# One attention loop over eight heads with a block of matmuls between any two steps, five PSUM banks for attention and three for the blocks

## The chip, the cores and the metric

The kernel runs on one core of one Trainium2 chip. The metric is the device time of the whole kernel in microseconds; three runs of the kernel before gave 1835.82 to 1836.56, median 1836.43.

## The reference, cut to the mixer

Two layers of an encoder run over 320 tokens: 256 of a prompt and 64 of a later step, side by side in one tile, in float32. A layer is SwiGLU, a mixer of three attentions, cross-attention to a memory, and a second SwiGLU, each with a layer norm behind it. The change touches the mixer:

```python
z = x @ w_in
(aq, ak, av, bq, bk, bv, iq, ik, iw, cq, ck, cv, gates) = split(z)
# A: chunk-band attention, 4 heads of 64, relative-position bias
ya = softmax(aq . ak / 8 + rel_bias) @ av
# B: top-k keys by the indexer's score, 4 heads of 64 on one shared K/V head
score = sum_h iw[h] * relu(iq[h] . ik);  sel = top_k(score)
yb = softmax(bq . bk[sel] / 8) @ bv[sel]
# C: differential attention, 4 heads of 2 x 64, headwise RMSNorm
a = softmax(cq[0] . ck[0] / 8) - lam * softmax(cq[1] . ck[1] / 8)
yc = rmsnorm(a @ cv) * subln_g * (1 - lam_init)
g_a, g_b, g_c = split(sigmoid(gates))
merged = g_a * (ya @ wb_a) + g_b * (yb @ wb_b) + g_c * (yc @ wb_c)
x = layer_norm(ALPHA * x + merged @ w_out)
```

## The kernel before, in words

A weight block is 128 x 1024 floats. `stream()` lists all blocks in the order of use. `nextw` hands out the next block and has `ahead(2)` prepare blocks until two more are ready: a DMA on SP's queue brings it into `raw`, ACT copies it to a rounded `hi` (L148), DVE subtracts to get `lo` (L151), both in two halves. `raw`, `hi` and `lo` have three buffers each. `block_mm` multiplies a block with the activations, which are split into high and low parts too: `mm3` (L183 to L185) issues three matmuls for each of eight pieces, so a block is 24 matmuls of 320 columns into one PSUM bank.

PSUM has eight banks. `psmm` takes from a group of four (`mm`, `PSM = 4`) for blocks, for the pairs of SwiGLU, for the memory's key and value projections that fill the norms (`fill_k`, `fill_v`), and for `proj_v`, which holds three at once. `psat` takes from the other four (`at`) for attention, for the norms' sums and for transposes. A bank is free again when ACT or DVE has read the tile.

The mixer (`attn_layer`) first projects values, indexer and the first keys and queries, computes the index scores, and then runs the loop. Eight steps of heads: two pairs of A heads, four C heads, two pairs of B heads. Each has scores (L633, two banks, then `softmax`: minima on DVE at L651 or L653, exp on ACT at L657, which for B and C heads reads the banks, a scaling on DVE at L665); a turn (L672, L674, L675: transposes into t0, t1 and `po`, three banks, read out at L681 to L683 or L818 and L819); values (L695 to L702 or L825 to L830, into `po`); for C heads a finish (L848, one bank, read at L851 and L852). Between the steps stand ten projections of queries and keys (`projs`, each with a rotation: L534 to L536 on DVE and POOL, L569 on POOL, and two steps of top-k, L777 and L778 on DVE) and six of the 24 gate blocks (`some_gates`, L787: tanh on ACT). Their order is written out by hand: some steps stand directly behind each other. The merge then goes over eight output blocks: three products of the branches with `wb` (A: 2 pieces, B: 2, C: 4), each scaled by its gate on DVE (L918), two adds on POOL (L919, L920), a split on ACT and DVE (L194, L195), and three more gate blocks behind each of the first six. Then comes the output projection (`wo`), whose results go into the residual (`Norm.resid`, L382 and L404), and with block 4 the norm starts its sums, between which `fill_k` or `fill_v` run; their results are read out late, at L298 or L328.

The program is laid out by a framework which fixes the order of each engine's instructions before the run, from the source's order and an estimate of when each can start, and places the semaphores. An engine then works its list strictly in order.

Of the kernel before, what the change touches and what calls it, by code (L numbers as in the profile page):

```python
# [10 lines left out]
F32 = mybir.dt.float32  # L11
# [42 lines left out]
QK1 = ([("aq", 0), ("ak", 0), ("aq", 1), ("ak", 1)]  # L54
       + [x for i in range(4) for x in (("cq", i), ("ck", i))] + [("bq", 0), ("bq", 1)])
QK = QK0 + QK1
EARLY = 2
TOPN = 2
NGATE = 10
NSLOT = 30  # L60
PSM = 4
FILL = ((8, 8, 4, 4), (4, 4, 0, 0))


def stream():
    for l in range(DEPTH):
        yield from ffn_stream(l, 0)
        for kc in range(4):
            yield ("wv0", l, kc), 656
        for q in QK0:  # L70
            yield ("wqk", l, QK.index(q)), D
        for h in range(4):
            yield ("wv1", l, h), D
        for q in QK1:
            yield ("wqk", l, QK.index(q)), D
        for g in range(EARLY * 3):
            yield ("wg", l, g), D
        for m in range(KB):
            yield ("wb", l, m), D
            for g in range((m + EARLY) * 3, min(m + EARLY + 1, KB) * 3):  # L80
                yield ("wg", l, g), D
        for n in ("wo", "wmq", "wmo"):
            for m in range(KB):
                yield (n, l, m), D
        yield from ffn_stream(l, 1)


def ffn_stream(l, which):
    for j in range(FB):
        for s in range(2):  # L90
            yield ("wgu", l, which, j, s), D
    for m in range(KB):
        for c0 in range(0, FB, 8):
            yield ("wd", l, which, m, c0), min(8, FB - c0) * 128
# [3 lines left out]
def encoder(ctx: ExitStack, tc: tile.TileContext, a):  # L98
# [29 lines left out]
    def psmm():  # L128
        return ps.tile([128, 512], F32, tag="mm", bufs=PSM, name="mm")

# [42 lines left out]
    def nextw(*key):  # L173
        ahead(1)
        k, w = ready.pop(0)
        assert k == key, (k, key)
        ahead(2)
        return w

    def mm3(out, w, x, k, kx, first, last):  # L180
# [124 lines left out]
    def fill_v(l, half):  # L305
        st = {}

        def mk(kc):
            def mm(w, ks):
                t = memT[0]  # L310
                if kc == 0 and 0 in ks:
                    st["p"] = [psmm() for _ in range(2)]
                for i in ks:
                    b, kk = i // 4, (i // 2) % 2
                    ts = slice(b * 128, (b + 1) * 128)
                    k = kc * 2 + kk
                    c = slice(kk * 512, (kk + 1) * 512)
                    p = st["p"][b]
                    if i % 2 == 0:
                        pe.matmul(p, t[:, 0, k, ts], w[0][:, c], start=(k == 0), stop=False)  # L320
                        pe.matmul(p, t[:, 1, k, ts], w[0][:, c], start=False, stop=False)
                    else:
                        pe.matmul(p, t[:, 0, k, ts], w[1][:, c], start=False, stop=(k == KB - 1))

                def out():
                    for b in range(2):
                        o = slot()[:, :512]
                        act.activation(o, st["p"][b], AF.Copy)  # L328
                        nc.sync.dma_start(a["omv"][l, :, b, half * 512:(half + 1) * 512], o)
                        c = half * D + b * 512  # L330
                        nc.sync.dma_start(mkv[l][:, 1, c:c + 512], o)
                if kc == 3 and 7 in ks:
                    late.append(out)
            return mm
        return [(a["wmv"][l, half * 4 + kc], mk(kc)) for kc in range(4)]
# [143 lines left out]
    def ffn(l, which, x, norm):  # L479
        h = []  # L480
        for j in range(FB):
            pg, pu = psmm()[:, :NT], psmm()[:, :NT]
            wg = nextw("wgu", l, which, j, 0)
            if j == 0 and not (l or which):
                for k in range(KB):
                    c = slice(k * 128, (k + 1) * 128)
                    pe.matmul(pg, wg[0][:, c], x[k][0], start=(k == 0), stop=False)
                    pe.matmul(pg, wg[0][:, c], x[k][1], start=False, stop=False)
                for k in range(KB):
                    c = slice(k * 128, (k + 1) * 128)  # L490
                    pe.matmul(pg, wg[1][:, c], x[k][0], start=False, stop=(k == KB - 1))
                wu = nextw("wgu", l, which, j, 1)
                for k in range(KB):
                    mm3(pu, wu, x, k, k, k == 0, k == KB - 1)
            elif j == 0:
                wu = nextw("wgu", l, which, j, 1)
                for k in range(KB):
                    mm3(pg, wg, x, k, k, k == 0, k == KB - 1)
                    mm3(pu, wu, x, k, k, k == 0, k == KB - 1)
            else:  # L500
                for k in range(KB):
                    mm3(pg, wg, x, k, k, k == 0, k == KB - 1)
                wu = nextw("wgu", l, which, j, 1)
                for k in range(KB):
                    mm3(pu, wu, x, k, k, k == 0, k == KB - 1)
            if l == 0 and which == 0 and j == 4:
                constants()
            if l == 0 and which == 0 and j == 6:
                load_mem()
            s = wtile()  # L510
            act.activation(s, pg, AF.Silu)
            dve.tensor_tensor(out=s, in0=s, in1=pu, op=OP.mult)  # L512
            h.append(pair())
            split(s, h[j])
        for m in range(KB):
            p = psmm()[:, :NT]
            for c0 in range(0, FB, 8):
                w = nextw("wd", l, which, m, c0)
                for k in range(min(8, FB - c0)):
                    mm3(p, w, h, k, c0 + k, c0 + k == 0, c0 + k == FB - 1)  # L520
            norm.resid(m, p)

    def attn_layer(l, x, norm):
# [255 lines left out]
                if not steps:  # L779
                    dve.tensor_scalar(hide, tk, MARK, None, op0=OP.is_gt)  # L780

        gates = []

        def gate(i):
            p = block_mm(nextw("wg", l, i), x)
            g = wk.tile([128, NT], F32, tag="gate", bufs=NGATE, name="gate")
            act.activation(g, p, AF.Tanh, scale=0.5)  # L787
            gates.append(g)

        def a_scores(hp):  # L790
            s, _ = scores(qk["aq", hp], qk["ak", hp])
            return softmax(s, bias=toep[:, hp])
# [60 lines left out]

        rest = [q for q in QK1[4:]]

        def projs(n):
            for _ in range(n):
                proj(*rest.pop(0))
                topk(TOPN)

        ng = [0]

        def some_gates(n):
            for _ in range(n):
                gate(ng[0])
                ng[0] += 1

        e0, e1 = a_scores(0), a_scores(1)
        projs(2)
        p0 = turn2(e0)  # L870
        projs(1)
        a_values(0, *p0)
        p1 = turn2(e1)
        projs(1)
        a_values(1, *p1)
        e0 = c_scores(0)
        projs(2)
        e1 = c_scores(1)
        projs(1)
        p0 = c_turn(e0)  # L880
        projs(1)
        w0 = c_values(0, *p0)
        e2 = c_scores(2)
        projs(1)
        p1 = c_turn(e1)
        projs(1)
        w1 = c_values(1, *p1)
        c_finish(0, w0)
        e3 = c_scores(3)
        some_gates(1)  # L890
        p2 = c_turn(e2)
        some_gates(1)
        w2 = c_values(2, *p2)
        c_finish(1, w1)
        e0 = b_scores(0)
        p3 = c_turn(e3)
        some_gates(1)
        w3 = c_values(3, *p3)
        c_finish(2, w2)
        e1 = b_scores(1)  # L900
        some_gates(1)
        p0 = turn2(e0)
        some_gates(1)
        b_values(0, *p0)
        p1 = turn2(e1)
        c_finish(3, w3)
        some_gates(1)
        b_values(1, *p1)
        some_gates(EARLY * 3 - ng[0])
        mg = []  # L910
        for m in range(KB):
            w = nextw("wb", l, m)
            gm = gates[3 * m:3 * m + 3]
            for b, (k0, n) in enumerate(((0, 2), (2, 2), (4, 4))):
                p = psmm()[:, :NT]
                for k in range(k0, k0 + n):
                    mm3(p, w, o, k, k, k == k0, k == k0 + n - 1)
                dve.scalar_tensor_tensor(gm[b], gm[b], 1.0, p, op0=OP.add, op1=OP.mult)  # L918
            pool.tensor_tensor(out=gm[0], in0=gm[0], in1=gm[1], op=OP.add)  # L919
            pool.tensor_tensor(out=gm[0], in0=gm[0], in1=gm[2], op=OP.add)  # L920
            mg.append(pair())
            split(gm[0], mg[m])
            for i in range((m + EARLY) * 3, min(m + EARLY + 1, KB) * 3):
                gate(i)
        load_mem()
        for m in range(KB):
            norm.resid(m, block_mm(nextw("wo", l, m), mg))
# [306 lines left out]
```

## Time and profile before

| | |
|---|---|
| median of three runs | 1836.43 us |
| the profiled execution | 1840.81 us |
| its span, first to last instruction | 1839.0 us |
| PE busy | 1768.6 us, 96% |
| DVE busy | 1173.5 us, 64% |
| ACT busy | 866.6 us, 47% |
| POOL busy | 279.5 us, 15% |
| DMA | 277.60 MB, 151 GB/s |

PE is the engine of the matmuls, PEld its loading of weights, DVE the vector engine, ACT the scalar engine, POOL GpSimd; SP only issues DMAs. Busy time of PE is the union of its instructions, whose ends are modelled. PEclk is the granted clock of TensorE: 1.00 is 2.4 GHz and 0.50 is 1.2 GHz. In a timeline row the bracket says how long the engine had been idle and what ended that. Times are us from the first instruction.

Layer 0's attention loop lies at 336 to 438.6 us, its merge behind it to 530, its output projection from there to 579; layer 1's loop lies at 1253.8 to 1356.5.

### The profile page before, as it was taken

How to read it: one execution, taken by the hardware profiler on the slowest of the kernel's cores; microseconds unless marked ns; L12 is line 12 of the kernel's file. 1: busy time of each engine (PE TensorE's matmuls, PEld its weight loads, DVE VectorE, ACT ScalarE, POOL GpSimd, SP SyncE). 2: the span in 40 equal slices, each digit the busy share in tenths (PEclk: the TensorE clock that was granted, in tenths of full speed). 3: DMA queues.
4: the chain of work that ended last, by engine and by line, in shares of the span. 5: the costliest groups of instructions: out<-in, count | busy, mean ns of one | idle time of the engine just before them, and what ended most of it. 6: DMA issues, size and time to landing. Idle time of an engine off the chain costs nothing. (4 is left out here: it accounts for less than half of the span.)

```text
span 1839.0 us, 31561 instructions
## 1 busy us (share of the span) xinstructions
PE 1768.6 (96%) x12148; PEld 1714.2 (93%) x12148; DVE 1173.5 (64%) x2274; ACT 866.6 (47%) x1939; POOL 279.5 (15%) x311
## 2 busy tenths in 40 slices
PE   8999999989998989999999999999899999899997
PEld 8999999979997989999999999999799989799996
DVE  5544667976567786444674446679765786844455
ACT  5444445555444655443444444455554455544433
POOL 1000122231123030000210001222311230400012
PEclk9999999999999999999999999999999999899998
DMA  6545645433556544445544445554334563354443
GB/s 223 172 150 146 197 143 184 144 108 115 150 171 214 170 140 132 149 150 154 181 136 150 149 144 156 163 173 150 102 121 154 162 199 100 105 160 149 147 126 101
DMA packets 93015, 277.60 MB, mean 151 GB/s; under 512 B 12480, under 2 KB 26688, under 8 KB 92352
## 3 DMA queue, kind: packets, MB, share of 16 engines
q1 hardware_dynamic: 85376, 268.64, 47.0%
q10 hardware_dynamic: 7488, 6.95, 1.3%
q8 instruction: 95, 1.56, 0.4%
q14 instruction: 56, 0.46, 0.1%
HBM read 260.67 MB, written 14.55 MB: 150 GB/s over the span
## 5 line engine op out<-in xcount | busy, mean ns | idle before, releaser
L183 PE MATMUL mm<-slot,hi 128*128 128x320 f32 x3368 | 1051.2, 312 | 17.4 <-ACT slot L472 7.9
L185 PE MATMUL mm<-slot,hi 128*128 128x320 f32 x3368 | 1043.9, 311 | 3.0 <-DVE slot L474 3.0
L184 PE MATMUL mm<-slot,lo 128*128 128x320 f32 x3368 | 1045.5, 311 | 0.5 <-DVE lo L151 0.4
L151 DVE TENSOR_TENSOR lo<-raw,hi 128x512 fp32r<-128x512 f32 (+2 forms) x876 | 616.1, 742 | 349.5 <-ACT hi L148 346.7
L148 ACT ACTIVATE hi<-raw 128x512 fp32r<-128x512 f32 (+2 forms) x876 | 496.2, 613 | 569.5 <-issue 343.2
L183 PEld LDWEIGHTS mm<-slot,hi 128*128 128x128 f32 x3368 | 636.9, 189 | 26.6 <-ACT slot L472 9.9
L185 PEld LDWEIGHTS mm<-slot,hi 128*128 128x128 f32 x3368 | 635.3, 189 | 6.7 <-DVE slot L474 6.2
L184 PEld LDWEIGHTS mm<-slot,lo 128*128 128x128 f32 x3368 | 636.6, 189 | 1.9 <-DVE lo L151 1.4
L386 POOL TENSOR_TENSOR acc<-x 128x320 f32<-128x320 f32 x8 | 10.0, 1254 | 850.4 <-DVE x L382 850.4
L512 DVE TENSOR_TENSOR w<-w,mm 128x320 f32<-128x320 f32 x88 | 42.9, 488 | 132.1 <-PE mm L185 126.4
L787 ACT ACTIVATE gate<-mm 128x320 f32<-128x320 f32 x48 | 21.0, 438 | 75.2 <-PE mm L185 75.2
L444 POOL TENSOR_TENSOR x<-x,msb 128x320 f32<-128x320 f32 x47 | 46.1, 1012 | 53.6 <-ACT msb L430 53.6
L377 POOL TENSOR_TENSOR acc<-acc,w 128x320 f32<-128x320 f32 x40 | 45.9, 1148 | 45.4 <-ACT w L371 44.6
L535 POOL TENSOR_TENSOR w<-w,cst 128x320 f32<-128x320 f32 x30 | 27.0, 898 | 165.0 <-DVE w L534 110.9
L472 ACT ACTIVATE slot<-w,vec 128x320 fp32r<-128x320 f32 x56 | 34.4, 649 | 35.2 <-DVE w L461 35.2
L376 POOL TENSOR_TENSOR acc<-acc,x 128x320 f32<-128x320 f32 x32 | 34.7, 1085 | 80.9 <-DVE x L404 80.1
L371 ACT ACTIVATE w<-x 128x320 f32<-128x320 f32 x64 | 28.4, 465 | 35.9 <-DVE x L404 26.2
L918 DVE SCALAR_TENSOR_TENSOR gate<-gate,mm 128x320 f32<-128x320 f32 x48 | 22.7, 483 | 32.5 <-PE mm L185 32.5
L195 DVE TENSOR_TENSOR slot<-w,slot 128x320 fp32r<-128x320 f32 x88 | 42.7, 485 | 0.5 <-ACT slot L194 0.5
L919 POOL TENSOR_TENSOR gate<-gate 128x320 f32<-128x320 f32 x16 | 14.1, 879 | 190.8 <-DVE gate L918 190.8
L194 ACT ACTIVATE slot<-w 128x320 fp32r<-128x320 f32 x88 | 40.2, 457 | 3.3 <-DVE w L512 3.2
L657 ACT ACTIVATE e<-at,st 128x192 f32<-128x192 f32 (+4 forms) x60 | 24.3, 422 | 35.6 <-DVE st L651 28.7
(238 smaller groups left out, 1621.9 us busy)
## 6 DMA issues: line engine op xcount, KB each, us to landing
raw<-wgu SPq DMA_DIRECT2D x175, 512.0 KB, 3.5
raw<-wd SPq DMA_DIRECT2D x64, 512.0 KB, 3.6
raw<-wg SPq DMA_DIRECT2D x48, 512.0 KB, 3.5
raw<-wqk SPq DMA_DIRECT2D x38, 512.0 KB, 3.6
raw<-wd SPq DMA_DIRECT2D x32, 384.0 KB, 3.5
raw<-wmk SPq DMA_DIRECT2D x16, 512.0 KB, 3.9
raw<-wb SPq DMA_DIRECT2D x16, 512.0 KB, 3.5
raw<-wo SPq DMA_DIRECT2D x16, 512.0 KB, 3.6
```

The lines of the kernel that those rows point to most:

```text
L148: act.activation(hi[:, c], raw[:, c], AF.Copy)
L151: dve.tensor_tensor(out=lo[:, c], in0=raw[:, c], in1=f(hi)[:, c], op=OP.subtract)
L183: pe.matmul(out, hi[:, c], x[kx][0], start=first, stop=False)
L184: pe.matmul(out, lo[:, c], x[kx][0], start=False, stop=False)
L185: pe.matmul(out, hi[:, c], x[kx][1], start=False, stop=last)
L194: act.activation(dst[0], src, AF.Copy)
L195: (eng or dve).tensor_tensor(out=dst[1], in0=src, in1=f(dst[0]), op=OP.subtract)
L376: eng.tensor_tensor(out=self.acc1, in0=x32[0] if m == 1 else self.acc1, in1=x32[m], op=OP.add)
L377: pool.tensor_tensor(out=self.acc2, in0=self.sq0 if m == 1 else self.acc2, in1=sq, op=OP.add)
L444: eng.tensor_tensor(out=x32[m], in0=x32[m], in1=msb, op=OP.subtract)
L472: act.activation(x[m][0], u, AF.Identity, scale=g, bias=b)
L512: dve.tensor_tensor(out=s, in0=s, in1=pu, op=OP.mult)
```

## The change

The banks are divided three (`PSM = 3`) to five. `fill_v` and the second half of each SwiGLU pair take theirs from the attention's five; in the merge branch B's product does too. The loop over heads is a real loop now: for each head a block, the next head's scores, a block, this head's turn, a block, this head's values, and for a C head the finish one head later. The blocks come from one list, `MIX`: P is a projection with its two steps of top-k, G a gate; ten P and fourteen G, against ten and six before. The first six gates lie in pairs in the slots of the large pool, the others in ten buffers as before; `gates_by(m)` says how many gates stand behind each output block of the merge: one behind the first, three behind the third to fifth, none behind the others. The merge takes the branches in the order A, C, B. Where the block just handed out is of `wqk`, `wg` or `wb`, the next one is copied to `hi` and `lo` whole and not in halves.

```diff
-EARLY = 2
+SGATE = 6
+EARLY = 14
+MIX = "PPGPPGPGPPGPGPPG" + "G" * 8
-PSM = 4
+PSM = 3
+def gates_by(m):
+    return min(3 * KB, max(3 * (m + 1), SGATE) + NGATE - 1) if m >= 0 else EARLY
...
-        ahead(2)
+        ahead(2, 1 if key[0] in ("wqk", "wg", "wb") else 2)
...
-                    st["p"] = [psmm() for _ in range(2)]
+                    st["p"] = [psat() for _ in range(2)]
...
-            pg, pu = psmm()[:, :NT], psmm()[:, :NT]
+            pg, pu = psmm()[:, :NT], psat()[:, :NT]
...
-            g = wk.tile([128, NT], F32, tag="gate", bufs=NGATE, name="gate")
+            if i < SGATE:
+                if i % 2 == 0:
+                    gslot[0] = slot()
+                g = gslot[0][:, (i % 2) * NT:(i % 2 + 1) * NT]
+            else:
+                g = wk.tile([128, NT], F32, tag="gate", bufs=NGATE, name="gate")
...
-        e0, e1 = a_scores(0), a_scores(1)
-        projs(2)
-        p0 = turn2(e0)
-        projs(1)
-        a_values(0, *p0)
-        p1 = turn2(e1)
-        projs(1)
-        a_values(1, *p1)
-        e0 = c_scores(0)
-        projs(2)
-        e1 = c_scores(1)
-        projs(1)
-        p0 = c_turn(e0)
-        projs(1)
-        w0 = c_values(0, *p0)
-        e2 = c_scores(2)
-        projs(1)
-        p1 = c_turn(e1)
...
-        b_values(1, *p1)
-        some_gates(EARLY * 3 - ng[0])
+        heads = ([(a_scores, turn2, a_values, i) for i in range(2)] + [(c_scores, c_turn, c_values, i) for i in range(4)]
+                 + [(b_scores, turn2, b_values, i) for i in range(2)])
+        e = heads[0][0](0)
+        fill(1)
+        done = None
+        for i, (_, turned, values, h) in enumerate(heads):
+            nxt = None
+            if i + 1 < len(heads):
+                fill(1)
+                nxt = heads[i + 1][0](heads[i + 1][3])
+            fill(1)
+            pt = turned(e)
+            fill(1)
+            w = values(h, *pt)
+            if done:
+                c_finish(*done)
+            done = (h, w) if values is c_values else None
+            e = nxt
+        fill(len(mix))
...
-            for b, (k0, n) in enumerate(((0, 2), (2, 2), (4, 4))):
-                p = psmm()[:, :NT]
+            for b, k0, n in ((0, 0, 2), (2, 4, 4), (1, 2, 2)):
+                p = (psat if b == 1 else psmm)()[:, :NT]
...
-            for i in range((m + EARLY) * 3, min(m + EARLY + 1, KB) * 3):
-                gate(i)
+            while len(gates) < gates_by(m):
+                gate(len(gates))
```

## Rows read from the trace of the kernel before

**Rows 1.** page, busy us (share of the span) x instructions, by engine
```profile
PE 1768.6 (96%) x12148; PEld 1714.2 (93%) x12148; DVE 1173.5 (64%) x2274; ACT 866.6 (47%) x1939; POOL 279.5 (15%) x311
```

**Rows 2.** windows: stretch, us, busy (x) PE PEld DVE ACT POOL, PEclk, DMA, GB/s
```profile
338.00:438.00 100.00, 91.30 (x698) 82.01 (x698) 77.67 (x223) 53.80 (x188) 27.84 (x42) 0.98 0.36 111
438.00:533.00 95.00, 95.00 (x648) 94.76 (x648) 57.22 (x96) 42.78 (x89) 14.68 (x16) 1.00 0.47 145
1256.00:1356.00 100.00, 90.04 (x698) 80.41 (x697) 77.68 (x223) 53.76 (x188) 27.57 (x40) 1.00 0.36 111
372.00:400.00 28.00, 22.34 (x170) 20.25 (x169) 22.94 (x60) 13.26 (x53) 13.16 (x20) 0.94 0.35 111
```

**Rows 3.** PE's waits: us, times, longest; loop of layer 0, then layer 1
```profile
PE at L675 <- ACT e L657: 5.1, 3, 3.0
PE at L674 <- DVE slot L852: 1.4, 1, 1.4
PE at L698 <- DVE pt L682: 1.2, 1, 1.2
PE at L825 <- DVE pt L819: 0.7, 1, 0.7
...
PE at L825 <- DVE pt L819: 2.0, 2, 1.3
```

**Rows 4.** timeline round one wait, layer 0: start, length, engine, line, operation
```profile
374.47 1.40 DVE L651 TENSOR_REDUCE st<-at 128x1 f32<-128x192 f32 x5
375.98 0.46 ACT L657 ACTIVATE e<-at,st 128x256 f32<-128x256 f32 x1
376.59 0.33 PE L675 MATMUL at<-cst,e 128*128 128x128 f32 x1 [3.04 <-ACT e L657]
378.60 0.67 ACT L818 ACTIVATE w<-at 128x256 f32<-128x256 f32 x2
380.11 1.00 DVE L819 TENSOR_TENSOR pt<-at,w 128x256 f32<-128x256 f32 x3
```

**Rows 5.** weight copies: page-like groups of ACT, then timeline of ACT and DVE
```profile
L148 ACT ACTIVATE e<-raw 128x1024 fp32r<-128x1024 f32 x22 | 23.1, 1056 | 20.2 <-DMA raw<-wmv 8.8 <-DMA raw<-wmk 8.3 <-PE mm L321 1.7
343.54 0.62 ACT L148 ACTIVATE hi<-raw 128x512 fp32r<-128x512 f32 x1
347.55 1.27 DVE L151 TENSOR_TENSOR lo<-raw,hi 128x512 fp32r<-128x512 f32 x1
```

**Rows 6.** timeline of DVE: the first top-k step of layer 0
```profile
322.76 0.36 DVE L777 MAX8 m<-tk 128x8 f32<-128x192 f32 x1
```

**Rows 7.** output projection: timeline of PE, layer 0 and 1, then a window
```profile
570.38 0.39 PE L183 MATMUL mm<-slot,hi 128*128 128x320 f32 x1 [1.21 <-DVE x L404]
1476.26 0.39 PE L183 MATMUL mm<-slot,hi 128*128 128x320 f32 x1 [2.10 <-DVE x L404]
1477.30:1480.60 3.30, 3.30 (x14) 3.30 (x13) 2.30 (x4) 2.33 (x5) 2.48 (x4) 0.50 0.97 362
```

**Rows 8.** value projection: timeline of PE and ACT, layer 0, then layer 1
```profile
273.44 0.42 PE L589 MATMUL mm<-hi,slot 128*128 128x328 f32 x1 [0.39 <-ACT w L298]
270.56 0.37 ACT L298 ACTIVATE w<-mm 128x256 f32<-128x256 f32 x1
273.03 0.63 ACT L298 ACTIVATE w<-mm 128x256 f32<-128x256 f32 x2
1191.31 0.42 PE L589 MATMUL mm<-hi,slot 128*128 128x328 f32 x1 [0.60 <-ACT slot L328]
```

**Rows 9.** last column of the merge: timeline of POOL and PE, layer 0
```profile
530.87 0.89 POOL L919 TENSOR_TENSOR gate<-gate 128x320 f32<-128x320 f32 x1 [2.49 <-DVE gate L918]
533.60 0.42 PE L183 MATMUL mm<-slot,hi 128*128 128x320 f32 x1 [0.17 <-ACT slot L194]
```

**Rows 10.** a block's last matmuls and its rotation: timeline, layer 0
```profile
357.26 0.31 PE L185 MATMUL mm<-slot,hi 128*128 128x320 f32 x1
361.21 0.53 DVE L534 STREAM_SHUFFLE w<-mm 128x320 f32<-128x320 f32 x1
```

More of the change, by code (lines that the diff above doesn't have):

```diff
@@ L73, in stream @@
             yield ("wv1", l, h), D
-        for q in QK1:
+        for q in QK1[:4]:
             yield ("wqk", l, QK.index(q)), D
-        for g in range(EARLY * 3):
-            yield ("wg", l, g), D
+        g, rest = 0, list(QK1[4:])
+        for c in MIX:
+            if c == "P":
+                yield ("wqk", l, QK.index(rest.pop(0))), D
+            else:
+                yield ("wg", l, g), D
+                g += 1
+        assert not rest and g == EARLY
         for m in range(KB):
             yield ("wb", l, m), D
-            for g in range((m + EARLY) * 3, min(m + EARLY + 1, KB) * 3):
+            for g in range(gates_by(m - 1), gates_by(m)):
                 yield ("wg", l, g), D
@@ L780, in topk @@
                     dve.tensor_scalar(hide, tk, MARK, None, op0=OP.is_gt)
-        gates = []
+        gates, gslot = [], [None]
         def gate(i):
             p = block_mm(nextw("wg", l, i), x)
-            g = wk.tile([128, NT], F32, tag="gate", bufs=NGATE, name="gate")
+            if i < SGATE:
+                if i % 2 == 0:
+                    gslot[0] = slot()
+                g = gslot[0][:, (i % 2) * NT:(i % 2 + 1) * NT]
+            else:
+                g = wk.tile([128, NT], F32, tag="gate", bufs=NGATE, name="gate")
             act.activation(g, p, AF.Tanh, scale=0.5)
@@ L854, in attn_layer, with fill @@
         rest = [q for q in QK1[4:]]
-        def projs(n):
+        mix = list(MIX)
+        def fill(n=1):
             for _ in range(n):
[L858 to L866, printed above, removed]
-        e0, e1 = a_scores(0), a_scores(1)
-        projs(2)
-        p0 = turn2(e0)
-        projs(1)
-        a_values(0, *p0)
-        p1 = turn2(e1)
-        projs(1)
-        a_values(1, *p1)
-        e0 = c_scores(0)
-        projs(2)
-        e1 = c_scores(1)
-        projs(1)
-        p0 = c_turn(e0)
-        projs(1)
-        w0 = c_values(0, *p0)
-        e2 = c_scores(2)
-        projs(1)
-        p1 = c_turn(e1)
[L886 to L907, printed above, removed]
-        b_values(1, *p1)
-        some_gates(EARLY * 3 - ng[0])
+                if mix.pop(0) == "P":
+                    proj(*rest.pop(0))
+                    topk(TOPN)
+                else:
+                    gate(len(gates))
[18 more added lines that the diff above has]
+        fill(len(mix))
         mg = []
@@ L922, in attn_layer @@
             split(gm[0], mg[m])
-            for i in range((m + EARLY) * 3, min(m + EARLY + 1, KB) * 3):
-                gate(i)
+            while len(gates) < gates_by(m):
+                gate(len(gates))
         load_mem()
```

## The prediction

> **What bounds the kernel now.** I read the page first: PE is busy for 96% of the span, DVE for 64% and ACT for 47% [rows 1], so only time that PE gets back counts. Next the table of windows, stage by stage, for where PE is not busy. In the merge stage that follows the attention loop it is busy for 95.00 of 95.00 us with 648 matmuls, which is 0.147 us a matmul and 3.52 us for a block of 24; weights come at 145 GB/s there without one wait [rows 2]. In the two loops PE is busy for 91.30 and 90.04 of 100 us: 8.70 + 9.96 = 18.7 us idle, the worst of it in a 28-us stretch where PE has 22.34 us [rows 2]. Third, PE's waits inside the loops: three at L675 for exp (5.1 us a layer), one at L674 for a head's finish (1.4), and waits for data at L698 and L825 [rows 3].
>
> What is the wait at L675? It is a transpose that reads a head's probabilities, long finished, and names the exp of *another* head. Its output needs a bank, and of four banks two hold the next head's scores and two hold t0 and t1. It starts at 376.59, just as the second of five exps (375.98 + 0.46) lets go of the first score bank, and those exps had to follow minima that DVE reached only at 374.47 [rows 4]. L674's wait is the same thing with c_finish's bank. So 6.5 us of each loop's idle time is a missing fifth bank; the rest is PE arriving at a step before ACT and DVE have brought the data [rows 3, 4].
>
> **Part 1, the loop.** No matmul is added or removed. Five banks are exactly next scores (2) + t0, t1, po (3). By the new order c_finish's bank and the previous po are read out while two blocks (7.0 us) run, so I find no point where a sixth is wanted: L675's and L674's waits go. The gap between a score and its own transpose becomes three blocks and one other head's steps, over 10.5 us, against a softmax of about 1.4 us minima, 2 us exps and 1.2 us scaling.
>
> What is late next is the data between transpose and value matmul, where one block (3.52 us) lies as before. In the row group of one such step, ACT's copies start at 378.60 and DVE's adds end at 381.11, 2.5 us of work, late only because the exps before them were late [rows 4]. The new a_scores(1) is moved behind two blocks, so that its DVE work no longer stands in front of head 0's copy (L698's wait). DVE has room: 77.67 us busy in the old loop [rows 2]; eight more gates in it add 8 x 3.52 = 28 us of PE and 8 x 1.27 us of DVE [rows 5], about 88 us of work in some 119 us. The top-k steps don't jam it: the order on each engine is laid down before the run, and they are taken up where DVE is free, from 322.76 on, before the loop [rows 6]. Bounds for what is left: none, up to the waits for data of before (1.9 us in layer 0, 3.2 in layer 1 [rows 3]); I take 1 us a layer, nearest to L825's one wait of 0.7 us.
>
> Gain: 18.7 us. Each of the 15 gaps also hides the tail of a matmul, which is shown 0.31 us long where the next starts 0.147 us later, 0.16 us each, 2.4 us. Over the 28-us stretch with the longest gaps of layer 0 TensorE's granted clock is 0.94 on the mean [rows 2]: 28 x 0.06 = 1.7 us. Sum 22.8, less 2: **20.8 us**.
>
> **Part 2, whole instead of half weight copies** after wqk, wg and wb blocks (102 a run). A whole 1024-column copy takes 1.06 us on ACT; a half takes 0.62, and PE could start on it [rows 5]. ACT and DVE time hardly changes. Cover: the copy is for the block two ahead, so 3.5 to 7 us of matmuls hide it, and no wait for hi or lo is among PE's waits in the loops [rows 3]. I cost it at nothing; uncovered it is 0.44 us a block. The Trainium skill, "Perfetto Trace Analysis", Optimizing Scalar/DVE Operations, speaks against this edit: an engine that isn't saturated but causes bubbles elsewhere should have its instructions broken up, so work completes sooner. The trace doesn't bear it out in this stage, where no bubble is a weight's; it is rival 4.
>
> **Part 3, three banks for the blocks.** Blocks are read out by ACT or DVE; with three banks the reader has two blocks, 7.0 us, of lead, where it had 10.5. The largest lag I find is a rotation whose block ended at 357.6 and whose shuffle ran at 361.21, 3.6 us [rows 10]: still covered. The SwiGLU pairs now take one bank of each kind, 3 and 5 deep instead of 2 pairs, and the memory projection's value fillers (fill_v) hold two attention banks instead of two of the block banks. Where fill_v runs under the output projection, only two banks were left for its blocks, and PE waited for a residual add: 1.21 us in layer 0, 2.10 in layer 1, with the clock at 0.50 (1.2 GHz) for 3.3 us behind it [rows 7]. With three, the last block but one no longer waits: 1.21 + 2.10 + two tails of 0.16 = 3.6 us, and half of the clock's 1.65, as that stretch has other waits that could lower it: 0.8. **Gain 4.4**; bounds 0 (if the norm behind it, which is DVE's, takes it back) and 5.3.
>
> Against that, at layer 0's value projection three key fillers hold banks; the one bank that was free is gone. proj_v takes three at once, its third group waited 0.39 us for the copies at L298, which end at 270.93, 273.4 and 273.7 [rows 8]. Now its first group gets the first of these, the second must wait from 272.0 to 273.5: 1.9 us lost instead of 0.55, **loss 1.3**. In layer 1 the fillers are values: the 0.60 us wait for L328 [rows 8] goes, **gain 0.6**.
>
> **Part 4, the merge.** Branch C before B gives the last head's output more time. But the first POOL add takes gates 0 and 1, and branch 1 is now last. For the last column the first add began at 530.87, behind two of three DVE products; now it follows the third, 0.4 us later, and the output projection already waits for that chain (0.17 us at 533.60 [rows 9]). **Loss 0.4 a layer, 0.8**; bounds 0 and 0.9 (the whole first add, 0.89) a layer. Gates 0 to 5 in free slots and the later gates' order cost nothing: the merge keeps 18 blocks for 8 outputs, DVE far from full (57 of 95 us with 27 blocks [rows 2]).
>
> **Sum**, against the profiled execution's 1840.81 us (its span of 1839.0 and 1.8 around it, which no step changes): 20.8 + 4.4 - 1.3 + 0.6 - 0.8 = 23.7, so 1817.1. Profiled runs stand 4.4 us above the median of the runs shown (1836.43); with the same difference the median comes to 1812.7, **1813 us**.
>
> **Rivals.** (1) *Data waits take the place of bank waits.* PE reaches each value step sooner, and ACT's exps of the next head stand in front of the evacuation. For: 1.9 and 3.2 us of such waits exist; against: part of them follows from late exps [rows 3, 4]. If all 16 value steps wait 0.7 us, L825's size in layer 0, that is 11.2 instead of 2: 1822 us.
>
> (2) *Blocks run out of banks: slower.* Place: the ten projection blocks of each loop, whose banks only DVE's shuffle and product free. From a lag of 7.0 us on PE waits. The lag seen is 3.6 [rows 10]; it would have to double. If each of 20 blocks then waits for one weight subtraction and one shuffle, 1.27 + 0.53 = 1.8 us [rows 5, 10], that is 36 us: 1849. Against: the projections now stand among gates, which ask nothing of DVE but weights. The Trainium skill's "Perfetto Trace Analysis", Matmuls, would have independent groups rotate through banks so that one's evacuation overlaps the next one's matmuls, which speaks for more banks here; the rows say that three rotate far enough.
>
> (3) *The order isn't what the source says.* Each engine's list is planned from estimates, and the planner may pull steps together again, as it pulled top-k forward [rows 6]. Then the loop gains nothing and only parts 3 and 4 stay, 2.9 us: 1834.
>
> (4) *Weights late: slower.* If each of 102 blocks waited for the second half of its copy, 102 x 0.44 = 45 us: 1858. Against: no such wait in the loops [rows 3].
>
> **How the numbers follow.** The forecast has 0.70, and its own range is 1807 (2 us more from the loop, 0.9 from part 3's clock, no loss in proj_v and at the chain: 1812.7 - 5.0 = 1807.7) to 1820 (the old data waits stay, 5.1 us instead of 2, and part 3's 4.4 is given back). Rival 1 has 0.20, rival 2 0.04, rival 3 0.04, rival 4 0.02. The range 1807 to 1826 holds the forecast and rival 1, whose upper end is 1822 with part 3's 4.4 given back. A difference under 0.2%, 3.7 us, is about what a measurement of this kernel can't tell from none. Faster by more: 0.70 + 0.20 + 0.01 of the partial cases of rival 3 = 0.91; within: 0.03 of rival 3 and 0.01 of mild cases of rival 2, 0.04; slower: 0.05.
>
> **What would show it.** In the windows over the new loops (about 28 us longer, as the gates move in) PE idle should be under 2 us each. L675 <- exp and L674 <- L852 should be gone from PE's waits; what is left should be L825 or L698, under 1 us each. In the output projection the waits for the residual add should be gone. proj_v of layer 0 should show a wait for L298 near 1.5 us, the first blocks of the output projection one near 0.6 us. Wrong would be: waits for a shuffle or a gate's read-out at a block's first matmul (rival 2), waits for hi or lo (rival 4), two steps with no block between them (rival 3), or idle time of 5 us or more a loop at value steps (rival 1).

## The result and the profile after

The changed kernel takes **1824.33 us** (median of four runs, 1823.31 to 1825.17) against 1836.49 beside it (1835.82 to 1839.82): ratio 0.993, interval 0.9913 to 0.9947. That is 12.2 us faster where 23.7 were forecast: right in direction and inside the range, with half the gain. The profiled execution took 1823.49 us, its span 1821.7, so the two profiled spans differ by 17.3. In the changed kernel `mm3` is L195 to L197, the weight copies L160 and L163, the split L206 and L207, the merge's product L910 and its POOL adds L911 and L912.

The page of after, busy us by engine; it answers [rows 1]:

```profile
PE 1765.1 (97%) x12148; PEld 1711.4 (94%) x12148; DVE 1150.2 (63%) x2172; ACT 855.7 (47%) x1837; POOL 299.3 (16%) x311
```

Windows over the two new loops of after and the start of its first output projection (columns of [rows 2]):

```profile
336.00:459.00 123.00, 121.73 (x937) 111.50 (x936) 87.00 (x221) 65.38 (x193) 28.69 (x42) 1.00 0.43 128
1244.60:1367.60 123.00, 121.66 (x937) 111.44 (x936) 86.95 (x221) 65.62 (x193) 28.38 (x40) 1.00 0.41 128
...
528.00:531.40 3.40, 3.04 (x12) 3.02 (x13) 2.61 (x4) 2.40 (x4) 0.00 (x0) 0.52 0.54 159
```

PE is idle for 1.27 and 1.34 us of each loop, where it was 8.70 and 9.96 [rows 2]. PE's waits in after (us, times, longest): the loop of layer 0, that of layer 1, then 460 to 600 us of layer 0.

```profile
PE at L707 <- ACT pt L695: 1.1, 2, 0.6
...
PE at L707 <- ACT pt L695: 1.2, 2, 0.7
...
PE mm L195 <- ACT slot L206: 2.8, 1, 2.8
PE at L335 <- DVE pt L163: 1.8, 1, 1.8
PE mm L195 <- ACT slot L484: 1.3, 2, 0.6
PE at L433 <- DVE w L207: 1.1, 1, 1.1
```

In the loops the waits went as forecast: of [rows 3] nothing is left but two waits for A's value copies. The waits at L335 (`fill_v`) and for L484 stood in the trace of before too, 1.5 and 1.3 us. But behind the merge stands a wait that was 0.17 us before [rows 9]. After's timeline, PE at the value projection, at the first output projection, and at the norm's sums of both layers:

```profile
273.47 0.42 PE L601 MATMUL mm<-hi,slot 128*128 128x328 f32 x1 [1.28 <-ACT w L310]
...
528.36 0.63 PE L195 MATMUL mm<-slot,hi 128*128 128x320 f32 x1 [2.81 <-ACT slot L206]
...
573.90 0.82 PE L433 MATMUL at<-w,onesR 128*128 128x320 f32 x3 [1.12 <-DVE w L207]
...
1436.80 0.41 PE L195 MATMUL mm<-slot,hi 128*128 128x320 f32 x1 [2.82 <-ACT slot L206]
...
1468.07 0.81 PE L433 MATMUL at<-w,onesR 128*128 128x320 f32 x3 [1.27 <-DVE w L207]
```

The first output block needs the eighth merged column split. After's POOL, DVE and ACT over the last columns of the merge in layer 0:

```profile
516.03 0.88 POOL L911 TENSOR_TENSOR gate<-gate 128x320 f32<-128x320 f32 x1 [11.38 <-DVE gate L910]
520.70 0.88 POOL L911 TENSOR_TENSOR gate<-gate 128x320 f32<-128x320 f32 x1 [1.97 <-DVE gate L910]
521.66 1.74 POOL L912 TENSOR_TENSOR gate<-gate 128x320 f32<-128x320 f32 x1
525.37 1.17 POOL L911 TENSOR_TENSOR gate<-gate 128x320 f32<-128x320 f32 x1 [1.97 <-DVE gate L910]
...
520.87 1.79 DVE L163 TENSOR_TENSOR lo<-raw,hi 128x1024 fp32r<-128x1024 f32 x1
523.93 0.49 DVE L207 TENSOR_TENSOR slot<-gate,slot 128x320 fp32r<-128x320 f32 x1 [1.27 <-ACT slot L206]
524.34 0.48 DVE L910 SCALAR_TENSOR_TENSOR gate<-gate,mm 128x320 f32<-128x320 f32 x1
524.74 0.48 DVE L910 SCALAR_TENSOR_TENSOR gate<-gate,at 128x320 f32<-128x320 f32 x1
...
523.43 0.47 ACT L206 ACTIVATE slot<-gate 128x320 fp32r<-128x320 f32 x1 [3.25 <-POOL gate L912]
```

Read it as a ring. The first POOL add starts at 520.70, the second at 521.66 and takes 1.74, ACT's L206 follows at 523.43, DVE's L207 at 523.93. Only behind L207 in DVE's list stand the next column's products of C and B (524.34, 524.74), and only behind B's the next first add, at 525.37. Once round is 0.96 + 1.77 + 0.50 + 0.41 + 0.40 + 0.63 = 4.67 us, and PE needs 3.52 for a column. With no gate block between them the last columns fall behind by 1.15 us each: twice (516.03 to 520.70 to 525.37) makes 2.3 of the 2.81.

### The profile page after: what moved, and what is told of

The parts are those of the page before. It is cut to its first block, busy times and chain, and to the rows that moved or that the text cites. A ratio compares the mean times of both kernels' runs of the same rounds, so it can differ in the third digit from the quotient of the medians.

```text
span 1821.7 us, 31329 instructions
## 1 busy us (share of the span) xinstructions
PE 1765.1 (97%) x12148; PEld 1711.4 (94%) x12148; DVE 1150.2 (63%) x2172; ACT 855.7 (47%) x1837; POOL 299.3 (16%) x311
## 4 chain that ended last, share of the span: by engine, by line
PE 87%; DVE 7%; ACT 2%; issue 1%; DMA 1%; POOL 1%; SPq 0%; DVEq 0%; POOLq 0%; ACTq 0%
PE mm L195 20%; PE mm L197 20%; PE mm L196 19%; PE at L195 6%; PE at L196 6%; PE at L197 6%; DVE w L473 1%; PE at L645 1%; DVE lo L163 1%; DVE x L456 1%; POOL gate L912 1%; DVE x L411 1%; DVE slot L486 0%; ACT hi L160 0%; DMA raw<-wo 0%
## 5 line engine op out<-in xcount | busy, mean ns | idle before, releaser
L195 PE MATMUL mm<-slot,hi 128*128 128x320 f32 x2632 | 823.2, 313 | 18.5 <-ACT slot L484 7.9
L197 PE MATMUL mm<-slot,hi 128*128 128x320 f32 x2632 | 815.6, 310 | 2.5 <-DVE slot L486 2.5
L196 PE MATMUL mm<-slot,lo 128*128 128x320 f32 x2632 | 815.9, 310 | 1.5 <-DVE lo L163 1.1
L163 DVE TENSOR_TENSOR lo<-raw,hi 128x512 fp32r<-128x512 f32 (+3 forms) x774 | 588.4, 795 | 344.9 <-ACT hi L160 341.5
L160 ACT ACTIVATE hi<-raw 128x512 fp32r<-128x512 f32 (+3 forms) x774 | 486.3, 669 | 561.6 <-issue 356.7
L195 PEld LDWEIGHTS mm<-slot,hi 128*128 128x128 f32 x2632 | 496.2, 189 | 29.2 <-ACT slot L484 9.9
L197 PEld LDWEIGHTS mm<-slot,hi 128*128 128x128 f32 x2632 | 495.6, 188 | 5.8 <-DVE slot L486 5.6
L196 PEld LDWEIGHTS mm<-slot,lo 128*128 128x128 f32 x2632 | 496.4, 189 | 3.2 <-DVE lo L163 2.8
L195 PE MATMUL at<-slot,hi 128*128 128x320 f32 x736 | 228.1, 310 | 0.0
L196 PE MATMUL at<-slot,lo 128*128 128x320 f32 x736 | 228.0, 310 | 0.0
L197 PE MATMUL at<-slot,hi 128*128 128x320 f32 x736 | 227.9, 310 | 0.0
L195 PEld LDWEIGHTS at<-slot,hi 128*128 128x128 f32 x736 | 138.9, 189 | 0.0
L196 PEld LDWEIGHTS at<-slot,lo 128*128 128x128 f32 x736 | 138.8, 189 | 0.0
L197 PEld LDWEIGHTS at<-slot,hi 128*128 128x128 f32 x736 | 138.6, 188 | 0.0
L484 ACT ACTIVATE slot<-w,vec 128x320 fp32r<-128x320 f32 x56 | 34.4, 650 | 35.7 <-DVE w L473 35.7
```

Of the source, the lines that this page charges most:

```text
L160: act.activation(hi[:, c], raw[:, c], AF.Copy)
L163: dve.tensor_tensor(out=lo[:, c], in0=raw[:, c], in1=f(hi)[:, c], op=OP.subtract)
L195: pe.matmul(out, hi[:, c], x[kx][0], start=first, stop=False)
L196: pe.matmul(out, lo[:, c], x[kx][0], start=False, stop=False)
L197: pe.matmul(out, hi[:, c], x[kx][1], start=False, stop=last)
L484: act.activation(x[m][0], u, AF.Identity, scale=g, bias=b)
```

## The experiments

Of the wait behind the merge there were two theories: **A**, the gates gone from behind the last three columns (only the last two had none before); **B**, the branch order, by which the first add waits for the last branch. Of the loops: the **bank theory**, that the fifth bank removed their waits, as predicted, and the **order theory**, that a block between any two steps did. Times are medians of up to eleven runs with the spread, and the ratio to the kernel before on the same chip.

**before_again**: the kernel before, unchanged, to see what its profiled execution held beyond a usual one.

> The kernel before, unchanged. Theory that the profiled execution was not typical: the executions differ by whole stretches of the lower clock, about 1.7 us each; a new profile near 1836 has one to three of them fewer than the first, the one in layer 0's loop among them, and the same waits of PE (8.4 us of bank and data waits in each loop). Rival, that the profile is right and the median of the new kernel carries something unseen: the new profile shows the same clock stretches as the first and about 1840 us. Time: 1836.5 in both, within 0.2% of the kernel before.

1837.11 us (1836.34 to 1841.23), ratio 1.0002 (0.9993 to 1.001). Its profile is of an execution of 1836.55 us with a span of 1834.8. PE's waits in the loop of layer 0, then in its output projection:

```profile
PE at L675 <- ACT e L657: 3.7, 3, 1.9
...
PE mm L183 <- DVE x L404: 0.5, 1, 0.5
```

The same waits as [rows 3] and [rows 7], but 1.4 us shorter at L675 in layer 0, and the residual's wait of 1.21 us is missing; the one of 0.5 us stands in both traces. Half-clock stretches of 3.4 us in the loop of layer 0, near 591 and near 1475 us are in both, and near 353 us this execution has one more. Fewer of them were expected here; up to the end of layer 1's mixer there are not. Against this execution the changed kernel's span gains 13.1 us.

**gates_spread**: the last ten gates lie one or two behind each of the first seven columns.

```diff
-    return min(3 * KB, max(3 * (m + 1), SGATE) + NGATE - 1) if m >= 0 else EARLY
+    return (15, 16, 18, 19, 21, 22, 24, 24)[m] if m >= 0 else EARLY
```

> The new kernel, with its last ten gates put 1, 1, 2, 1, 2, 1, 2 behind output columns 0 to 6 of the merge instead of 1, 0, 3, 3, 3, 0, 0. Theory A, the column's chain: three columns back to back go at the pace of DVE, POOL, ACT, DVE (4.67 us a column by POOL's rows) against 3.53 us of matmuls, and the output projection pays for the lag (2.8 us a layer); with a gate between them the wait falls under 0.6 us a layer, and with it goes the clock stretch behind it in layer 0: 1824.3 - 4.5 to 6 = 1818 to 1820. Theory B, branch order alone: the wait stays at 2.8 us, and 1824.

**1814.38 us** (1811.32 to 1818.12), ratio 0.9874 (0.9859 to 0.989), the lowest median of all. The first output block in its trace:

```profile
526.38 0.42 PE L195 MATMUL mm<-slot,hi 128*128 128x320 f32 x1 [0.31 <-ACT slot L206]
```

0.31 us for 2.81, and the stretch at half clock behind it is gone too. These 0.31 us and the 2.3 of the ring make 2.6 of the 2.81. In layer 1's output projection a wait for a weight's low part (PE L196 for DVE's L163) that the changed kernel hasn't takes 0.99 us back, in order_abc 1.71 and in pool_c_first 1.86. Theory A holds; the gain is more than expected, 10 us from median to median and 5.3 in span (its profiled execution was the slowest of its four).

**order_abc**: only the merge's order goes back to A, B, C.

```diff
-            for b, k0, n in ((0, 0, 2), (2, 4, 4), (1, 2, 2)):
+            for b, k0, n in ((0, 0, 2), (1, 2, 2), (2, 4, 4)):
```

> The new kernel with the merge's branches in the old order A, B, C. Theory A: the chain of a column is shorter by at most one POOL add (0.9 us) in the last column, the pace of the three columns before stays over 3.53 us: the wait falls from 2.8 to about 2 us a layer, 1822 to 1823. Theory B: the wait falls to the 0.2 us of before, 1818 to 1819. If branch B's early place makes PE wait for the last head's output, up to 1 us a layer is lost at the merge's start.

1817.87 us (1816.37 to 1821.0), ratio 0.9894 (0.9879 to 0.991). Its POOL over the same columns:

```profile
515.08 0.88 POOL L911 TENSOR_TENSOR gate<-gate 128x320 f32<-128x320 f32 x1 [12.17 <-DVE gate L910]
519.02 0.89 POOL L911 TENSOR_TENSOR gate<-gate 128x320 f32<-128x320 f32 x1 [2.02 <-DVE gate L910]
519.98 0.88 POOL L912 TENSOR_TENSOR gate<-gate 128x320 f32<-128x320 f32 x1
522.89 0.88 POOL L911 TENSOR_TENSOR gate<-gate 128x320 f32<-128x320 f32 x1 [2.02 <-DVE gate L910]
```

A column now takes 3.94 and 3.87 us, and PE doesn't wait for L206 at all. So theory B holds as well: the lag is a product of two factors, columns that follow another without a gate, and 1.15 us for each of them.

**pool_c_first**: the order stays A, C, B, but POOL adds C first, then B.

```diff
-            pool.tensor_tensor(out=gm[0], in0=gm[0], in1=gm[1], op=OP.add)
             pool.tensor_tensor(out=gm[0], in0=gm[0], in1=gm[2], op=OP.add)
+            pool.tensor_tensor(out=gm[0], in0=gm[0], in1=gm[1], op=OP.add)
```

> The new kernel, with POOL adding branch C to A first and B last, so that the first add can start while B's matmuls run. Theory A: each column's chain is shorter by up to one add (0.9 us), so 4.67 becomes about 3.8 us a column, still over 3.53: the wait falls to about 0.5 to 1 us a layer, 1820 to 1822. Theory B: the wait falls to 0.2 us, 1818 to 1819. If the chain isn't it, 1824.

1818.64 us (1817.49 to 1821.75), ratio 0.9899 (0.9886 to 0.9913). Its POOL over the same columns:

```profile
517.60 0.88 POOL L911 TENSOR_TENSOR gate<-gate 128x320 f32<-128x320 f32 x1 [2.02 <-DVE gate L910]
518.56 0.88 POOL L912 TENSOR_TENSOR gate<-gate 128x320 f32<-128x320 f32 x1
521.47 0.88 POOL L911 TENSOR_TENSOR gate<-gate 128x320 f32<-128x320 f32 x1 [2.02 <-DVE gate L910]
```

A column takes 3.87 us twice; the wait is gone in both layers. So it is which product the first add waits for, not the order on PE, that makes the ring too long. Two things change with it: B's product leaves the ring (1.02 us from L207 to the next first add, for 1.44), and the second add now starts ahead of the subtraction of a weight block and not into it (0.88 us for 1.74), so that ACT's L206 starts 0.92 us behind its start and not 1.77. Against that, L207 comes 0.47 us later, behind that subtraction. order_abc shows the same short second add. No run separates the two.

**spread_c_first**: both edits together.

> Gates spread behind the output columns as in gates_spread, and POOL adding C first. Theory A, the column's chain: the last wait of gates_spread at the output projection, 0.31 us a layer, goes too, and nothing else: 1813 to 1815. If the two edits remove the same time twice, as the theory says, the gain over the new kernel is that of gates_spread (10) plus at most 1, not the sum of the two (16).

1815.88 us (1814.76 to 1816.81), ratio 0.9884 (0.987 to 0.9897). No more than gates_spread alone: either cure takes the whole wait.

**sub_on_pool**: the column's last subtraction goes from DVE to POOL, so that the next products don't stand behind it.

```diff
-            split(gm[0], mg[m])
+            split(gm[0], mg[m], pool)
```

> The new kernel, with the subtraction that ends each output column of the merge on POOL instead of DVE, the gates where the new kernel has them. Theory A says that a column takes 4.67 us because DVE's products of the next column stand in its list behind the subtraction of this one, which waits for POOL and ACT: with the subtraction off DVE the last columns go at the pace of the matmuls, 3.5 to 3.6 us by POOL's first adds, and the wait at the output projection falls from 2.8 to 0.5 to 1.3 us (POOL's subtraction is some 0.5 us slower than DVE's): 1819 to 1822. If the pace is POOL's own (its adds take 0.9 to 1.7 us each here), more work on POOL makes it slower: over 4.7 us a column and over 1825.

1823.24 us (1821.32 to 1823.82), ratio 0.992 (0.9908 to 0.9933). POOL, and PE at the first output block:

```profile
519.99 0.88 POOL L911 TENSOR_TENSOR gate<-gate 128x320 f32<-128x320 f32 x1
520.95 1.74 POOL L912 TENSOR_TENSOR gate<-gate 128x320 f32<-128x320 f32 x1
523.27 0.89 POOL L207 TENSOR_TENSOR slot<-gate,slot 128x320 fp32r<-128x320 f32 x1 [0.58 <-ACT slot L206]
524.11 1.33 POOL L911 TENSOR_TENSOR gate<-gate 128x320 f32<-128x320 f32 x1
...
527.26 0.41 PE L195 MATMUL mm<-slot,hi 128*128 128x320 f32 x1 [1.93 <-ACT slot L206]
```

DVE's place in the ring is taken by POOL, which has no idle time left in it but 0.58 us for ACT: 4.12 us a column, still over 3.52. The wait only falls to 1.93 us, and POOL's slower subtraction adds 0.35 of its own. That is neither of the cases expected: the place on DVE's list is part of the ring, and POOL's own work, the second add of 1.74 us among it, is most of what is left.

**loop_four_banks**: the new order and all else, but the banks divided four to four as before.

```diff
-PSM = 3
+PSM = 4
-                    st["p"] = [psat() for _ in range(2)]
+                    st["p"] = [psmm() for _ in range(2)]
-            pg, pu = psmm()[:, :NT], psat()[:, :NT]
+            pg, pu = psmm()[:, :NT], psmm()[:, :NT]
-                p = (psat if b == 1 else psmm)()[:, :NT]
+                p = psmm()[:, :NT]
```

> The new loop, merge and weight copies with the old division of the banks, four and four, fill_v and SwiGLU on the blocks' four. Theory of the fifth bank: next scores hold two banks, t0 and t1 two, so L675 waits for exp and L674 for the finish as before, 4 to 6.5 us a layer; the output projection waits for the residual add again (1 to 2 us a layer), proj_v of layer 0 gets 1.3 us back: 1824.3 + 10 = 1832 to 1837. Rival, the order does it: a block now lies between the next head's scores and the turn, and 3.5 us hide the minima and the exps that free the first score bank, so L675 waits under 1 us a turn, 3 us a layer at most: 1826 to 1829.

1826.69 us (1826.26 to 1827.65), ratio 0.9942 (0.9929 to 0.9956). PE's waits in the loop of layer 0, then at the output projection of layer 1:

```profile
PE at L687 <- ACT e L669: 0.9, 1, 0.9
PE at L687 <- DVE st L665: 0.7, 1, 0.7
...
PE mm L195 <- DVE x L416: 2.2, 1, 2.2
```

With four banks the loop waits 1.5 us at its turns (0.85 and 0.69), with five 1.1 at its values. The residual wait of [rows 7] is back in layer 1, but not in layer 0.

**banks_alone**: the old loop, merge and copies with the new division of the banks.

```diff
-PSM = 4
+PSM = 3
-                    st["p"] = [psmm() for _ in range(2)]
+                    st["p"] = [psat() for _ in range(2)]
-            pg, pu = psmm()[:, :NT], psmm()[:, :NT]
+            pg, pu = psmm()[:, :NT], psat()[:, :NT]
-                p = psmm()[:, :NT]
+                p = (psat if b == 1 else psmm)()[:, :NT]
```

> The kernel before with five and three banks (fill_v, half of each SwiGLU pair and branch B's product on the five), its loop, merge and copies as they were. Theory of the fifth bank: L675's and L674's waits, 6.5 us a layer, go: with the output projection's 3.5 us won and proj_v's 1.3 lost, 1837 - 15 = 1820 to 1824. Rival, the order does it: the turn no longer waits, but the values then wait for copies and adds that stand behind the exps on ACT and DVE; half or more of it comes back at L825 or L698: 1826 to 1831.

1832.7 us (1831.61 to 1835.66), ratio 0.9979 (0.997 to 0.9988). Timeline of PE in the loop of layer 0, then a window behind the first of its waits:

```profile
380.79 0.80 PE L825 MATMUL at<-slot,pt 128*128 128x128 f32 x2 [3.97 <-DVE pt L819]
394.97 0.49 PE L825 MATMUL at<-slot,pt 128*128 128x128 f32 x2 [1.03 <-DVE pt L819]
406.96 0.49 PE L825 MATMUL at<-slot,pt 128*128 128x128 f32 x2 [0.31 <-DVE pt L819]
412.75 0.33 PE L675 MATMUL at<-cst,e 128*128 128x128 f32 x1 [1.00 <-DVE slot L852]
...
378.80:386.00 7.20, 5.21 (x34) 4.26 (x35) 6.76 (x14) 2.82 (x13) 4.53 (x7) 0.53 0.35 129
```

L675's waits for exp are gone, and what they held back waits at L825: 5.3 us where L675 had 5.1 [rows 3], with the clock at 0.53 behind the longest. The kernel is 4.1 us faster than the one before beside it, less than either theory expected, and its loop 1.0 us shorter (the rows stand in part 1 below), where the bank theory expected 6.5: this theory falls. The Trainium skill, "Perfetto Trace Analysis", Optimization Strategy, says that the same gap repeating on the engine that should be saturated can mean too little room in SBUF or PSUM; here the row named a bank, and the room gave 1.0 us a loop.

**halves**: the whole weight copies go back to two halves.

```diff
-        ahead(2, 1 if key[0] in ("wqk", "wg", "wb") else 2)
+        ahead(2)
```

> The new kernel with all weight copies in halves, as before. If whole copies cost nothing, as forecast: within 2 us of 1824. If the rule of broken-up instructions held and whole copies came late, faster by waits for hi or lo that should then be seen in the profile of the new kernel, which shows none in the loops. In the chain of a column, halves could let the planner put DVE's products earlier: the wait of the output projection may move by 1 us either way, not more.

1822.53 us (1822.01 to 1822.8), ratio 0.992 (0.9907 to 0.9932), 1.8 us under the changed kernel, with intervals that overlap. The loop of layer 0, window and waits:

```profile
336.00:459.00 123.00, 122.45 (x944) 112.91 (x937) 91.92 (x250) 69.61 (x223) 26.34 (x42) 1.00 0.43 129
...
PE at L710 <- DVE pt L694: 0.6, 1, 0.6
```

PE gets back 0.7 us of idle time in the loop, and one of the two waits at the values is gone. From its first score to its last value matmuls the loop takes 120.79 us, 1.2 less than in the changed kernel.

**spread_halves**: gates_spread with copies in halves.

> Gates spread as in gates_spread, and all weight copies in halves. The new kernel with halves was 1.8 us faster than with whole copies, mostly in two waits of the A heads (0.7 us each) that became one of the same size, in both layers. If that is independent of the gates: 1814.4 - 1.8 = 1812.6, 1811 to 1814.5. If whole copies lost their time in the merge's tail instead, nothing is left to win here: 1814.4.

1816.5 us (1814.35 to 1817.37), ratio 0.9888 (0.9873 to 0.9903): not under gates_spread, though its profiled span, 1812.6, is the shortest. The 1.2 us a loop shows in the trace again (120.78 for 121.94 in gates_spread), but these medians can't tell it from nothing.

**spread_four_banks**: gates_spread with the banks four to four.

> Gates spread as in gates_spread, with the old division of the banks, four and four, everywhere. The runs so far say that the order of the loop and not the fifth bank removes the waits: then this loses against gates_spread (1814.4) only what the new kernel with four banks lost against the new kernel (2.4 us: the residual add's wait in layer 1, 2.2, and small waits, less 0.9 in proj_v): 1815 to 1818. If the fifth bank did matter where the gates stand later, the loops would wait for exp again: over 1820.

1820.37 us (1815.63 to 1821.58), ratio 0.9903 (0.9889 to 0.9916). PE in the output projection of layer 1:

```profile
1457.67 0.39 PE L195 MATMUL mm<-slot,hi 128*128 128x320 f32 x1 [3.13 <-DVE x L416]
```

The median is over the 1820 us that were named for loops waiting for exp again, but the loops wait 1.5 us each as in loop_four_banks. The spans differ by 3.5 us, the loops by 0.6 each, this one wait by 3.1; the value projection gives 0.9 back. So the new division is worth a few microseconds, most of them at the output projection. How many stays open: the two ratios touch.

## Why the prediction was half right

Where each stage starts on PE, in the two profiled executions: to layer 0's value projection -0.3 us gained, from there to the first sum of the norm behind its mixer (L392 before, L404 after) 5.8, from there to layer 1's value projection 2.0, to its first sum 8.3, to the end 1.4; together 17.3.

**Part 1, the loop: near in size, wrong in cause.** PE's first score and last value matmuls in the loop of layer 0: before, banks_alone, loop_four_banks, after.

```profile
335.96 1.96 PE L633 MATMUL at<-slot 64*64 64x320 f32 x40
438.15 0.48 PE L702 MATMUL at<-pt,slot 64*128 64x128 f32 x2
...
335.62 1.96 PE L633 MATMUL at<-slot 64*64 64x320 f32 x40
436.80 0.48 PE L702 MATMUL at<-pt,slot 64*128 64x128 f32 x2
...
335.93 1.09 PE L645 MATMUL at<-slot 64*64 64x320 f32 x20
458.46 0.48 PE L714 MATMUL at<-pt,slot 64*128 64x128 f32 x2
...
336.46 1.09 PE L645 MATMUL at<-slot 64*64 64x320 f32 x20
458.42 0.48 PE L714 MATMUL at<-pt,slot 64*128 64x128 f32 x2
```

From start to start that is 102.19, 101.18, 122.53 and 121.96 us, and within 0.1 the same in layer 1; the last two hold eight gate blocks more, 28.2 us. So the loops gained 8.4 and 8.3 us, 16.7 where 20.8 were forecast. That is little more than the idle time that PE got back, 18.7 less 2.6; of the 4.1 us added for tails and clock hardly any shows. The leftovers are 1.1 and 1.2 us of waits, at L707 rather than L825 or L698.

But the step "6.5 us of each loop's idle time is a missing fifth bank" failed. The new order with four banks gains 7.8 us a loop; the fifth bank gains 1.0 under the old order and 0.6 more under the new one. The size came near because the order did what the bank was meant to do, and that is luck. The row at L675 did name a bank. What held that bank was an exp waiting for late minima, and the same exps stand on ACT's list in front of the copies for this head's values: in banks_alone the minima start at 374.10, the exps end at 377.22, a weight copy at 378.35, and the adds (L819) that the values wait for start at 379.74, behind a scaling and a rotation on DVE. With more room PE only came earlier to the next step that it wasn't ready for. That was rival 1's mechanism, true of the banks alone.

The mixer stretches, 5.8 and 8.3 us, hold less than the loops gained, since the merge took 2.6 from each and the value projection 0.9 and the clock 1.1 from layer 0. They also hold two gains that no term named: 0.7 and 0.9 us between value projection and loop, apart from the 0.60 us of [rows 8], and a wait of PE at the norm's first sum in before,

```profile
PE at L392 <- POOL some L389: 1.2, 1, 1.2
```

1.0 in layer 1. It is gone in after, and in loop_four_banks too, so it isn't the banks'. In layer 0 DVE's third residual add stands, before, behind the subtraction of a filler's weight (544.44 behind 543.30), and in after ahead of it (537.46 and 538.04); why the planner turned the two around stays open.

**Part 2, whole copies: nearly nothing, not nothing.** 1.2 us a loop by the trace, 2.4 in all, which the medians don't settle. "No wait for hi or lo" holds; the price is paid by the attention steps behind a copy on ACT's list: in after a whole copy of 1.05 us (352.67) stands right in front of the read-outs L693 and L695 that the values at 354.55 wait for. The rule cited in the prediction against this edit points the right way, with a small number.

**Part 3: the waits went as said, what they gave did not.** The value projection waits 1.28 us, near the 1.5 named, for L310, which is L298 of before. The residual's waits are gone; only in layer 1 do they come back with four banks. But the norm behind took much of that back, the lower bound of this term: its sums now wait 1.12 and 1.27 us for DVE's L207. From the norm's first sum to its end, with the half-clock stretch that followed before, the profiled pair gains 1.5 us in layer 0 and 2.0 in layer 1, 3.5 for the 4.4 of the forecast; against before_again, with its shorter wait, it gains 0.4 and 2.0.

**Part 4, the merge: the step that failed.** "Loss 0.4 a layer", with a bound of 0.9, was 2.6 a layer, and 1.1 us of clock behind it in layer 0 (from the wait to L404 PE takes 12.42 us there and 11.33 in layer 1): 6.4 instead of 0.8. I priced the branch order on the last column alone and said that "the later gates' order cost nothing", for DVE's load over the whole stage. What counted was the ring through POOL, ACT and DVE for one column. Before, it was already longer than PE's 3.52 us (the first add of the column ahead of [rows 9] began at 526.46, 4.41 us earlier), but only the last two columns ran without gates. The change made it 4.67 us, and took away a gate block that had let it catch up.

**From the profile to the median.** 23.7 less 5.6 in the merge is 18.1, not far from the 17.3 of the two spans. That is luck in part: the loops gave 4.1 less, and 3.7 came from the norm's first sum and from the stretches ahead of the loops. The other 5 us were in the step "with the same difference the median comes to": before's profiled execution stood 4.4 us over its median, after's 0.8 under. before_again, 4.2 us shorter in span, shows where that lay: 1.1 us up to layer 0's value projection, where the change does nothing, 1.4 between layer 0's first norm sum and layer 1's value projection (the residual's wait above all), and 1.4 behind layer 1's mixer (a half-clock stretch of 10.2 us instead of 13.7). The loops hardly differ, 102.16 and 102.19 us in layer 0: what L675 waits less there, another half-clock stretch takes. So part 3's term was read from an execution that had it in full, and the rest of the shift was never the change's to keep.

Of the rivals, none was the case: blocks never waited for a read-out of their banks (2), the steps stand apart (3), no block in the loop waited for weights (4), and rival 1's 0.7 us at every value step was 1.1 us a layer. The time lies outside the forecast's own range, 1807 to 1820; it is inside the whole one because that was drawn up to 1826 for rival 1. That rival 1's 1822 us lie nearer than the forecast is chance.

## What to carry to other kernels

A wait that names a full buffer is only worth a buffer if what made its holder late doesn't also stand in front of the next step's data; ask what that was. Where one chain crosses several engines once for each step, add up the ring from start to start, list order included, and compare it with the time that the busiest engine gives a step: filler work between the steps hides a ring that is too long, and moving the filler brings it out with the number of bare steps as its factor. Put the sum against two executions of the kernel before, since one may hold waits that the median hasn't.

## What the runs showed of the hardware

POOL's add of 320 columns takes 0.88 us alone and 1.74 beside DVE's subtraction of a whole weight block: the add issued at 521.66 into the subtraction of 520.87 to 522.66 ended at 523.40, 0.74 us after it, and ACT's L206, which waits for it, starts at 523.43. The Trainium skill, "SBUF — State Buffer", Who interferes with whom, says that a VectorE operation with two SBUF inputs contends with a GpSimd operation that reads SBUF, and that the ports they share are locked and not divided; these rows agree.

TensorE fell to 1.2 GHz (granted clock 0.52 over 3.4 us) behind the 2.81 us wait of layer 0, and stayed at 2.4 GHz behind the same wait, 2.82 us, of layer 1: the window from 1432 to 1440 has 1.00. A wait's price in clock can't be read from its length alone.
